# State-space weights made in the feed-forward block, untiled output products, and a weight block between all steps of the last attention

## The chip, the cores and the metric

The kernel runs on one core of one Trainium2 chip. The metric is device time in microseconds (us). The engines are PE (matrix products; PEld is its weight load), DVE (vector), ACT (scalar), POOL (GpSimd) and SP, which issues most transfers. SBUF is the memory beside the engines, PSUM the one that PE writes.

## The reference

The input is 512 tokens of 1024 features in float32. Two blocks follow each other, each of two layers. The first block (`block1`) mixes two attentions with gated projections. A layer of the second block is three residual steps: a gated feed-forward step of inner width 2816 (step 0), a token mixer (step 1), a second feed-forward step (step 2), each between RMS norms scaled by a vector made from `c`.

The mixer projects to `u` (512 wide), `q`, `k`, `v` (512 each), a forget logit and two gates. Its first branch is a state-space layer:

```python
lam_bar = jnp.exp(lam * dt)
b_bar = ((lam_bar - 1.0) / lam)[..., None] * b
bu = jnp.einsum('blgn,gpn->blgp', uf.astype(jnp.complex64), b_bar)
_, states = lax.associative_scan(combine, (a_all, bu), axis=1)
y = jnp.real(jnp.einsum('gnp,blgp->blgn', c, states)) + d_skip * uf
```

It has 32 groups of 16 channels with 64 complex states each. `gelu(y) @ glu_w` is split in a value and a gate. The second branch is a causal attention of 8 heads with a forget bias. Both branches are gated, added and projected.

## The kernel before

Every large product keeps float32 accuracy by three products of float32r parts: activations and weights are each split in a high part and a residual (`mm3`, lines 340 to 342; `tokens`, lines 417 to 419). A weight block of 128x1024 is loaded by SP (line 320), ACT makes its high part (line 323) and DVE its residual (line 324). Three buffers each hold raw, high and low parts; other tiles of up to 128x1024 share the buffers called `big`, 34 of them.

The program is written as Python generators that interleave work, and a planner orders each engine's instructions from that text and from estimated costs when the kernel is built. On the chip each engine follows its own list in that order.

A feed-forward step (`ffn`) runs over the 22 inner chunks of 128 in passes of 8, 7 and 7 (`SPLIT_K`). In a pass each chunk takes two weight blocks (`mblock`, 48 products of 512 columns) and an activation chain: tanh on ACT (line 1059), two DVE operations (1060, 1061), the high part on ACT (429), the residual on DVE or POOL (432). The pass ends with `tokens` for four groups of 128 tokens, whose results are added to `y` by DVE (1083). Between these, `pump` steps the job that makes the scaling vectors (line 1005, `modw` loads).

After pass 0 of step 0, `ssm_params` computes the small tables of the state-space layer. The mixer (`mixer`) projects `u` and `q`, then walks `fox_in` (forget logit, `k`, `v`) and `fox` (the attention). After every step of these, `side` advances three things: the state-space generator `ssm`, the 16 gate blocks in pairs, and, late, the 8 gated products (`gated`).

`ssm` treats the 512 tokens as 128 blocks of four (j = 0..3) and the channels in four quarters q. Per quarter it does this:

- DVE makes `bl`, the discretised input weights, in six operations (lines 1229 to 1234); PE turns them (line 1254) and ACT and DVE copy the result to `gt`.
- POOL makes `cl`, the output weights times powers of the transition (lines 1224, 1266, 1269), and `cs`, cosines and sines (1229 to 1234 with POOL as the engine).
- PE makes `kt`, the kernel within a block (1284, 1287), masked by DVE (1290).
- PE multiplies `u` by `gt` (1298); DVE and POOL rotate, DVE scans (1309, 1310), DVE and POOL rotate back to `hh`.
- PE makes the output in `yps`: four products with `kt` (1329) and 32 with 32 columns of `cl` each (1334). A tanh form of gelu follows (1338 to 1342), then the split in two parts (`gl`).

`halves_qk` (lines 561 to 573) splits a pair of heads for the scores (PE lines 579, 580) at the start of each pair.

## Time and profile before

| | |
|---|---|
| median of 3 runs | 3258.12 us (3255.19 to 3262.57) |
| profiled execution | 3255.03 us |
| its span, first to last instruction | 3253.0 us |
| mean granted clock of PE | 0.991 |

The span is what the rows are taken from; 2.0 us of the profiled execution lie around it. Busy time of an engine is not what limits the kernel by itself: it has to be read stage by stage, with what each engine waits for.

### The profile page before, as it was taken

The page shows a single profiled execution, that of the slowest core. Times are in us where ns is not written, and L with a number is a line of the kernel's source. Part 1 is how long each engine was busy: PE and PEld are TensorE (multiplying, and loading weights), DVE is VectorE, ACT ScalarE, POOL GpSimd, SP SyncE. Part 2 cuts the span into 40 slices and gives each one's busy share as a digit, 9 for nine tenths or more (in the row PEclk, how much of TensorE's full clock was granted, in tenths as well). Part 3 has the DMA queues.
Part 4 walks back from the last instruction along what each step waited for, and adds up shares of the span by engine and source line. Part 5 has one row for each costly group of instructions (what it writes and reads, how often), then busy time and mean ns, then how long its engine had stood idle before and what let it go on. Part 6 is the DMA issues. An engine that isn't in the chain of part 4 may idle for free. (4 is left out here: it accounts for less than half of the span.)

```text
span 3253.0 us, 41737 instructions
## 1 busy us (share of the span) xinstructions
PE 3159.7 (97%) x15958; PEld 2571.7 (79%) x15958; DVE 1961.7 (60%) x3525; ACT 1209.4 (37%) x2082; POOL 519.3 (16%) x578
## 2 busy tenths in 40 slices
PE   9999999999999999998999999999999989999999
PEld 8777888778788888876778888888888767788887
DVE  5897756887856848577565533634345776653334
ACT  4446423455333314433443222432234334442312
POOL 1200132000230101354001000100003451010000
PEclk9999999999999999999999999999999999999999
DMA  4243532233526537321233632332233211322323
GB/s 166 82 148 102 182 133 80 88 132 115 210 85 207 197 119 247 98 91 40 72 130 105 200 104 97 137 110 82 94 136 105 82 56 56 133 94 97 128 66 109
DMA packets 133464, 383.15 MB, mean 118 GB/s; under 512 B 15072, under 2 KB 21776, under 8 KB 133264
## 3 DMA queue, kind: packets, MB, share of 16 engines
q1 hardware_dynamic: 132208, 377.31, 34.2%
q0 software_dynamic: 1056, 3.17, 0.3%
q8 instruction: 126, 2.06, 0.3%
q14 instruction: 74, 0.61, 0.1%
HBM read 361.52 MB, written 18.90 MB: 117 GB/s over the span
## 5 line engine op out<-in xcount | busy, mean ns | idle before, releaser
L340 PE MATMUL acc<-big,wh 128*128 128x512 f32 (+1 forms) x2760 | 1074.4, 389 | 6.1 <-DVE tmp L725 2.9
L341 PE MATMUL acc<-big,wh 128*128 128x512 f32 (+1 forms) x2760 | 1068.9, 387 | 0.7 <-POOL big L517 0.7
L342 PE MATMUL acc<-big,wl 128*128 128x512 f32 (+1 forms) x2760 | 1066.1, 386 | 1.0 <-DVE wl L324 1.0
L324 DVE TENSOR_TENSOR wl<-raw,wh 128x1024 fp32r<-128x1024 f32 x396 | 500.7, 1267 | 527.9 <-ACT wh L323 511.9
L323 ACT CAST wh<-raw 128x1024 fp32r<-128x1024 f32 x396 | 414.1, 1046 | 978.6 <-issue 469.3
L340 PEld LDWEIGHTS acc<-big,wh 128*128 128x128 f32 x2760 | 521.2, 189 | 119.0 <-PE acc L342 5.3
L342 PEld LDWEIGHTS acc<-big,wl 128*128 128x128 f32 x2760 | 521.3, 189 | 109.0 <-DVE wl L324 1.4
L341 PEld LDWEIGHTS acc<-big,wh 128*128 128x128 f32 x2760 | 521.1, 189 | 103.6 <-POOL big L517 1.1
L1005 DVE SCALAR_TENSOR_TENSOR ms<-ms,big 128x512 f32<-128x512 f32 x288 | 199.6, 718 | 44.3 <-DMA ms<-in_modw_dram 43.7
L432 POOL TENSOR_TENSOR big<-tmp,big 128x512 fp32r<-128x512 f32 (+1 forms) x44 | 69.8, 1587 | 814.5 <-ACT big L429 814.5
L1061 DVE SCALAR_TENSOR_TENSOR tmp<-tmp,acc 128x512 f32<-128x512 f32 (+1 forms) x88 | 57.2, 650 | 149.9 <-PE acc L342 149.6
L429 ACT ACTIVATE big<-tmp 128x512 fp32r<-128x512 f32 (+1 forms) x148 | 88.1, 595 | 148.7 <-POOL tmp L881 56.3
L324 DVE TENSOR_TENSOR big<-raw,big 128x1024 fp32r<-128x1024 f32 x92 | 115.0, 1262 | 13.2 <-ACT big L323 12.5
L417 PE MATMUL acc<-big,big 128*128 128x512 f32 x288 | 113.1, 393 | 0.0
L419 PE MATMUL acc<-big,big 128*128 128x512 f32 x288 | 113.0, 392 | 0.0
L418 PE MATMUL acc<-big,big 128*128 128x512 f32 x288 | 112.9, 392 | 0.0
L605 ACT ACTIVATE big<-att,sm 128x512 f32<-128x512 f32 (+2 forms) x112 | 69.5, 624 | 116.6 <-DVE sm L603 116.4
L419 PE MATMUL att<-big,big 128*128 128x512 f32 x288 | 112.4, 390 | 0.0
L417 PE MATMUL att<-big,big 128*128 128x512 f32 x288 | 112.2, 390 | 0.0
L418 PE MATMUL att<-big,big 128*128 128x512 f32 x288 | 112.1, 389 | 0.0
L323 ACT CAST big<-raw 128x1024 fp32r<-128x1024 f32 x92 | 94.7, 1044 | 45.1 <-DMA raw<-in_w_dram 45.1
L482 ACT ACTIVATE hf<-big 128x512 f32<-128x512 f32 x80 | 50.3, 629 | 136.0 <-DVE big L1096 80.7
(395 smaller groups left out, 5102.4 us busy)
## 6 DMA issues: line engine op xcount, KB each, us to landing
raw<-in_w_dram SPq DMA_DIRECT2D x486, 512.0 KB, 3.3
ms<-in_modw_dram SPq DMA_DIRECT2D x288, 256.0 KB, 3.8
xb2l0s<-big SPq DMA_DIRECT2D x12, 512.0 KB, 2.7
big<-xb2l0s SPq DMA_DIRECT2D x12, 512.0 KB, 7.0
xb1l<-big SPq DMA_DIRECT2D x8, 512.0 KB, 2.6
big<-xb1l SPq DMA_DIRECT2D x8, 512.0 KB, 6.3
xb2l1s<-big SPq DMA_DIRECT2D x8, 512.0 KB, 2.6
big<-xb2l1s SPq DMA_DIRECT2D x8, 512.0 KB, 7.0
```

Source lines behind the costliest of these rows:

```text
L323: nc.scalar.copy(hi[:, :n], raw[:, :n])
L324: nc.vector.tensor_tensor(lo[:, :n], raw[:, :n], hi[:, :n].bitcast(F32), op=ALU.subtract)
L340: nc.tensor.matmul(ps, lhsT=hi, rhs=a, start=first, stop=False)
L341: nc.tensor.matmul(ps, lhsT=hi, rhs=b, start=False, stop=False)
L342: nc.tensor.matmul(ps, lhsT=lo, rhs=a, start=False, stop=last)
L417: nc.tensor.matmul(ps[m], lhsT=a, rhs=hi, start=c == o[0], stop=False)
L418: nc.tensor.matmul(ps[m], lhsT=a, rhs=lo, start=False, stop=False)
L419: nc.tensor.matmul(ps[m], lhsT=b, rhs=hi, start=False, stop=c == o[-1])
L429: nc.scalar.activation(hi, src, AF.Copy, scale=scale)
L432: eng.tensor_tensor(lo, src, hi.bitcast(F32), op=ALU.subtract)
L605: nc.scalar.activation(ps[j], s_ps[j], AF.Exp, bias=ng[:, j:j + 1], scale=scale, accum_out=rs[:, j:j + 1])
L1005: nc.vector.scalar_tensor_tensor(w, in0=w, scalar=0.5, in1=self.sc[m], op0=ALU.mult, op1=ALU.mult, accum_out=sums[:, n, m:m + 1])
```

## The change

1. `ssm_prep` makes the state-space weights inside feed-forward step 0 of the same layer. All three complex products (`bl`, `cl`, `cs`) are now on DVE. The finished tiles go to DRAM (`ssd`) by transfers that POOL issues, 11 per quarter. The generator has 40 steps: in pass 0 and pass 3 one step follows each chunk, in passes 1 and 2 two, and two follow each token group.
2. Step 0 runs in passes of 5, 5, 5 and 7; `pump` there does half as many job steps after a chunk.
3. The kernel within a block is stored as a 128x128 triangle of 32x32 blocks per group of 32 channels, so that the output needs 12 products of 128x128 per quarter. The gelu's result goes to DRAM and back (`yd`), five transfers from POOL, to return to the order of the tokens.
4. `ssm` in the mixer loads five tiles per quarter by SP and keeps only the work that needs `u`.
5. `fox` yields after each pair of score blocks, 24 times in all, and `fill` puts one gate block or gated product after each; `fox_in` is followed only by `ssm` steps. `halves_qk` for the next pair is called earlier.
6. `big` has 37 buffers; the memory for them comes from the scratch of POOL's transfers, set to 2048.

```diff
-SPLIT_K = (8, 7, 7)
+SPLIT_K = ((5, 5, 5, 7), (8, 7, 7))
-MIX = (1, 3, 1, 16)
-BUFS = dict(raw=3, wh=3, wl=3, big=34, tmp=5, hf=3, ms=5, s16=8, pw=1, pr=1, acc=3, att=2, aux=2, yps=1, mod=2, sums=1)
+BUFS = dict(raw=3, wh=3, wl=3, big=37, tmp=5, hf=3, ms=5, s16=8, pw=1, pr=1, acc=3, att=2, aux=2, yps=1, mod=2, sums=1)
...
-    c[:, C_BLK:C_BLK + 128] = (q // 32 == k // 32).astype(f)
+    c[:, C_BLK:C_BLK + 128] = (q % 32 == k).astype(f)
...
-        for p, n in enumerate(SPLIT_K):
+        prep = self.ssm_prep(l) if i == 0 else iter(())
+        for p, n in enumerate(SPLIT_K[i // 2]):
...
-                self.pump(2)
+                for _ in range(1 if p % 3 == 0 else 2):
+                    next(prep, None)
+                self.pump(1 if i == 0 else 2)
...
-            if p < len(SPLIT_K) - 1:
+            if p < len(SPLIT_K[i // 2]) - 1:
...
                     self.pump()
+                    for _ in range(2):
+                        next(prep, None)
...
-                if i == 0:
-                    self.ssm_p = self.ssm_params(l)
+        for _ in prep:
+            pass
...
+        P.update(rho=r[:, 3], tc=tc_, ts=ts_, l=(lr, li), f=(fr, fi))
+
+    def ssm_prep(self, l):
...
+        P = {}
+        for _ in self.ssm_params(l, P):
+            yield 1
...
+        s4 = [128, 4, 8, 16]
+        self.ssd[l] = ssd = self.dr.tile([4, 4, 128, 1024], F32, name=f"ssd{l}")
+        t = self.big()
+
+        def cplx(o, a, b, c, d, view, sign):
+
+            plus = (ALU.subtract, ALU.add)[::sign]
+            for k, x, y in ((0, c, d), (1, d, c)):
+                v.tensor_tensor(view(o[:, k]), a, x, op=ALU.mult)
+                v.tensor_tensor(view(t[:, k]), b, y, op=ALU.mult)
+                v.tensor_tensor(o[:, k], o[:, k], t[:, k], op=plus[k])
+                yield 1
+
+        def store(i, o, eng=g):
+            eng.dma_start(ssd[q, i], o.rearrange("p a b -> p (a b)"))
 
         for q in range(4):
             pq = slice(q * 4, q * 4 + 4)
             bk = self.big()
-            bc, kt = v3(bk[:, 0]), v3(bk[:, 1])
+            bc = bk[:, 0].rearrange("p (a b) -> p a b", a=4)
+            kt = bk[:, 1, 0:128].rearrange("p (a b) -> p a b", a=4)
             nc.sync.dma_start(bk[:, 0], self.io["ssmbc"][l, q])
...
+            for _ in cplx(bl, b0, b1, f0, f1, lambda x: x.rearrange("p (a b c) -> p a b c", a=4, b=4), 1):
+                yield 1
...
+            nc.scalar.mul(bc[:, 3], bc[:, 3], -1.0)
+            cl = self.big()
...
+            for _ in cplx(cl, l0, l1, c0, c1, lambda x: x.rearrange("p (a b c) -> p a b c", a=4, b=4), -1):
+                yield 1
+            store(1, cl)
+            yield 1
...
-            nc.scalar.mul(bc[:, 3], bc[:, 3], -1.0)
-            cl = self.big()
-            t = self.big()
...
-            mul(v4(t[:, 0]), cv[1], lv[1])
...
+            store(0, gt)
+            yield 1
             cs = self.big()
...
-            cplx(g, cs, *ta, *tb, lambda t: t.rearrange("p (a b c) -> p a b c", a=4, b=8))
...
+            it = cplx(cs, *ta, *tb, lambda x: x.rearrange("p (a b c) -> p a b c", a=4, b=8), 1)
+            yield next(it)
...
+            ps = self.t("aux", [128, 512])
+            for i in range(4):
+                s = slice(i * 32, i * 32 + 32)
+                for c in range(2):
+                    w = bb[:, c * 128 + i * 32:c * 128 + i * 32 + 32]
+                    nc.tensor.matmul(ps[s, 0:32], lhsT=w, rhs=bc[:, 2 + c, s], start=c == 0, stop=c == 1)
+                for c in range(2):
+                    w = bb[:, c * 128 + i * 32:c * 128 + i * 32 + 32]
+                    nc.tensor.matmul(ps[s, 32:128], lhsT=w, rhs=cl[:, c, i * 128:i * 128 + 96],
+                                     start=c == 0, stop=c == 1)
+            nc.scalar.copy(bk[:, 1, 0:128], ps[:, 0:128])
+            yield next(it)
+            store(2, cs)
+            v.scalar_tensor_tensor(kt[:, 0], in0=self.cst[:, C_BLK:C_BLK + 32],
+                                   scalar=self.par[l][:, P_SD + q:P_SD + q + 1],
+                                   in1=kt[:, 0], op0=ALU.mult, op1=ALU.add)
+            rho = ru[:, 0].rearrange("p (a b) -> p a b", a=4)
             nc.scalar.copy(rho, P["rho"][:, pq].unsqueeze(2).to_broadcast([128, 4, 128]))
             g.memset(rho[:, :, 0:1], 0.0)
-            nc.sync.dma_start(ru[:, 1], ud[q])
+            tri = ssd[q, 3, :, 0:512].rearrange("p (i x) -> p i x", i=4)
+            for j in range(4):
+                js = slice(j * 32, j * 32 + 32)
+                g.dma_start(tri[js, :, j * 32:].rearrange("e i x -> i e x"), bk[:, 1, 0:128 - j * 32])
+                if j:
+                    g.dma_start(tri[js, :, 0:j * 32],
+                                self.cst[js, C_BLK + 32:C_BLK + 32 + j * 32].unsqueeze(1).to_broadcast([32, 4, j * 32]))
+            g.dma_start(ssd[q, 3, :, 512:1024], ru[:, 0])
             yield 1
-            ps = self.t("aux", [128, 512])
-            for c in range(2):
-                nc.tensor.matmul(ps[:, 0:128], lhsT=bb[:, c * 128:(c + 1) * 128], rhs=bc[:, 2 + c],
-                                 start=c == 0, stop=c == 1)
-            for c in range(2):
-                nc.tensor.matmul(ps[:, 128:512], lhsT=bb[:, c * 128:(c + 1) * 128], rhs=cl[:, c, 0:384],
-                                 start=c == 0, stop=c == 1)
...
-            v.tensor_tensor(kt, v3(ps), blk, op=ALU.mult)
...
+    def ssm(self, l, ud, out):
...
+        def load(q):
+
+            ts = [self.big() for _ in range(4)]
+            for i, t in enumerate(ts):
+                nc.sync.dma_start(t.rearrange("p a b -> p (a b)"), self.ssd[l][q, i])
+            uu = self.big()
+            nc.sync.dma_start(uu[:, 1], ud[q])
+            return *ts, uu
+
+        for q in range(4):
+            gt, cl, cs, kr, uu = load(q)
+            ct, st = cs[:, 0], cs[:, 1]
+            yield 1
...
             yield 1
+            yield 1
-            uq = u[q // 2][:, q % 2]
-            for a in range(4):
-                n = (4 - a) * 128
-                nc.tensor.matmul(y_ps[:, a * 128:], lhsT=kt[:, a], rhs=uq[:, :n], start=a == 0, stop=False)
-            for j in range(4):
-                o = y_ps[:, j * 128:(j + 1) * 128]
+            for i in range(4):
+                s = slice(i * 128, (i + 1) * 128)
+                nc.tensor.matmul(y_ps[:, s], lhsT=kr[:, 0, s], rhs=uu[:, 1, s], start=True, stop=False)
                 for c in range(2):
-                    for i in range(4):
-                        nc.tensor.matmul(o[i * 32:(i + 1) * 32], lhsT=cl[:, c, j * 128 + i * 32:j * 128 + i * 32 + 32],
-                                         rhs=hh[:, c, i * 128:(i + 1) * 128], start=False, stop=j == 3 and c == 1)
+                    nc.tensor.matmul(y_ps[:, s], lhsT=cl[:, c, s], rhs=hh[:, c, s], start=False, stop=c == 1)
...
-            out.append(self.split(q2.rearrange("p (j k) -> p k j", j=4), scale=0.5, view="p (k j) -> p k j"))
+
+            g.dma_start(yd[q], q2)
+            d = yd[q].rearrange("(j e) (i k) -> j e i k", j=4, i=4)
+            for i in range(4):
+                g.dma_start(uu[i * 32:(i + 1) * 32, 0].rearrange("e (j k) -> e j k", j=4),
+                            d[:, :, i].rearrange("j e k -> e j k"))
+            yield 1
+            out.append(self.split(uu[:, 0].rearrange("p (j k) -> p k j", j=4), scale=0.5, view="p (k j) -> p k j"))
             yield 1
...
+        def fill():
+
+
+            for j in range(8):
+                t = self.big()
+                tg.append(t)
+                for k in range(2):
+                    ps = self.mblock(self.wk("gate"), h)
+                    nc.scalar.activation(t[:, k], ps, AF.Tanh, scale=0.5)
+                    yield 1
+            for _ in S_:
+                pass
...
-        def side(i):
-
-            while side.s * MIX[0] < i + 1 and next(S_, None):
-                side.s += 1
-            while len(tg) < 8 and len(tg) * MIX[1] < i + 1:
-                tg.append(self.g_pair(h))
-            while len(gl) == 4 and side.g < len(tg) and side.g * MIX[2] < i + 1 - MIX[3] and next(G_, None):
-                side.g += 1
...
+        S_ = self.ssm(l, ud, gl)
+        F_ = fill()
         next(S_)
-        n = 0
-        for it in (self.fox_in(l, h, st), self.fox(st, yb)):
-            for _ in it:
-                side(n)
-                n += 1
-        for _ in S_:
-            pass
-        for _ in G_:
+        for n, _ in enumerate(self.fox_in(l, h, st)):
+            for _ in range(1 + n % 2):
+                next(S_, None)
+        for n, _ in enumerate(self.fox(st, yb)):
+            next(F_, None)
+            next(S_, None)
+        for _ in F_:
             pass
...
+        ahead = self.halves_qk(qf[0][:, 0], kf[0][:, 0])
         for hp in range(4):
-            qk = self.halves_qk(qf[hp // 2][:, hp % 2], kf[hp // 2][:, hp % 2])
+            qk = ahead
...
-                    if q == 2:
-                        yield 1
+                    if q and e and hp < 3:
+                        n = hp + 1
+                        ahead = self.halves_qk(qf[n // 2][:, n % 2], kf[n // 2][:, n % 2])
+                    yield 1
...
-    nc = bacc.Bacc("TRN2", target_bir_lowering=False, num_devices=1)
+    nc = bacc.Bacc("TRN2", target_bir_lowering=False, num_devices=1, dynamic_dma_scratch_size=2048)
```

## Rows read from the trace of the kernel before

**Rows 1.** The page, its first part: busy time, share of the span, instructions.

```profile
PE 3159.7 (97%) x15958; PEld 2571.7 (79%) x15958; DVE 1961.7 (60%) x3525; ACT 1209.4 (37%) x2082; POOL 519.3 (16%) x578
```

**Rows 2.** Windows by stage: feed-forward 0, mixer, of each layer; columns in the prediction.

```profile
922.80:1300.60 377.80, 374.70 (x1763) 311.24 (x1763) 244.01 (x581) 121.03 (x176) 44.27 (x64) 0.99 0.52 178
1300.60:1713.50 412.90, 389.42 (x2204) 311.57 (x2203) 275.73 (x385) 170.57 (x311) 119.11 (x109) 0.98 0.25 85
...
2086.20:2458.50 372.30, 371.55 (x1763) 308.56 (x1762) 164.00 (x318) 119.09 (x174) 33.91 (x47) 1.00 0.32 106
2458.50:2875.30 416.80, 391.92 (x2204) 311.69 (x2203) 275.51 (x381) 170.35 (x311) 118.45 (x109) 0.98 0.25 84
```

**Rows 3.** Waits of PE in the mixer of layer 0: total us, times, longest.

```profile
PE aux L1254 <- DVE big L1231: 5.7, 2, 3.4
PE att L580 <- DVE big L573: 3.9, 1, 3.9
PE aux L1254 <- DVE big L1234: 3.5, 2, 2.4
...
PE att L579 <- DVE big L570: 1.9, 1, 1.9
PE aux L1254 <- ACT big L928: 1.6, 1, 1.6
```

**Rows 4.** The same view, mixer of layer 1.

```profile
PE aux L1254 <- DVE big L1231: 6.6, 2, 3.5
PE aux L1254 <- DVE big L1234: 5.2, 3, 3.1
...
PE att L580 <- DVE big L573: 2.5, 1, 2.5
...
PE aux L1254 <- ACT big L928: 1.9, 1, 1.9
```

**Rows 5.** Windows of 10 us, the nine at a lower clock: first and last.

```profile
1400.00:1410.00 10.00, 6.97 (x26) 5.11 (x24) 10.00 (x7) 1.05 (x1) 10.00 (x7) 0.83 0.18 61
...
2690.00:2700.00 10.00, 8.73 (x40) 6.41 (x41) 9.58 (x17) 1.86 (x6) 3.08 (x3) 0.83 0.16 52
```

**Rows 6.** Timeline of PE, layer 0: start us, duration us, instruction.

```profile
1360.96 2.05 PE L1298 MATMUL att<-big,big 128*128 128x128 f32 x16
...
1363.08 0.39 PE L341 MATMUL acc<-big,wh 128*128 128x512 f32 x1
1363.31 0.39 PE L342 MATMUL acc<-big,wl 128*128 128x512 f32 x1
```

**Rows 7.** Timeline of PE, one quarter's output products, layer 1.

```profile
2545.31 2.32 PE L1329 MATMUL yps<-big,big 128*128 128x512 f32 x8
2548.21 0.43 PE L1334 MATMUL yps<-big,big 128*32 128x128 f32 x8 [0.57 <-DVE big L1322]
2548.80 1.74 PE L1334 MATMUL yps<-big,big 128*32 128x128 f32 x56 [0.17 <-DVE big L1323]
```

**Rows 8.** Lines 1231 and 1234, whole run: duration ns min/median/max, first, last.

```profile
L1231 DVE TENSOR_TENSOR big<-big,big x8: 1480/1562/1747, 1347.7 to 2666.3; 128x512 f32<-128x512 f32 x8
...
L1234 DVE TENSOR_TENSOR big<-big,big x8: 676/1538/1770, 1352.9 to 2672.4; 128x512 f32<-128x512 f32 x8
```

**Rows 9.** Groups by line, DVE, feed-forward 0 of layer 0.

```profile
L1005 DVE SCALAR_TENSOR_TENSOR ms<-ms,big 128x512 f32<-128x512 f32 x108 | 77.6, 749 | 27.5 <-DMA ms<-in_modw_dram 27.3
L324 DVE TENSOR_TENSOR wl<-raw,wh 128x1024 fp32r<-128x1024 f32 x50 | 62.0, 1242 | 43.9 <-ACT wh L323 43.4
...
L1060 DVE SCALAR_TENSOR_TENSOR tmp<-tmp,acc 128x512 f32<-128x512 f32 (+1 forms) x22 | 14.2, 644 | 4.9 <-ACT tmp L1059 4.9
```

**Rows 10.** Line 1029, a transfer issued from POOL.

```profile
L1029 POOL DMA_DIRECT2D gates<-tmp x6: 587/600/747, 1065.8 to 3013.5; - x6
...
DMA to landing us min/median/max: 1.6/1.7/1.8
```

More of the change, by code (lines that the diff above doesn't have):

```diff
@@ L1208, in ssm_params @@
             v.tensor_tensor(fi[:, :, j], d1, d2, op=ALU.add)
-        return dict(rho=r[:, 3], tc=tc_, ts=ts_, l=(lr, li), f=(fr, fi))
-    def ssm(self, l, P, u, ud, out):
+        P.update(rho=r[:, 3], tc=tc_, ts=ts_, l=(lr, li), f=(fr, fi))
+    def ssm_prep(self, l):
         nc = self.nc
         v, g = nc.vector, nc.gpsimd
+        P = {}
+        for _ in self.ssm_params(l, P):
+            yield 1
         d4 = [128, 4, 4, 32]
-        def v4(t):
-            return t.rearrange("p (a b c) -> p a b c", a=4, b=4)
-        def v3(t):
-            return t.rearrange("p (a b) -> p a b", a=4)
-        def mul(o, a, b):
-            g.tensor_tensor(o, a, b, op=ALU.mult)
-        def cplx(e, o, a, b, c, d, view):
-            t = self.big()
-            e.tensor_tensor(view(o[:, 0]), a, c, op=ALU.mult)
-            e.tensor_tensor(view(t[:, 0]), b, d, op=ALU.mult)
-            e.tensor_tensor(o[:, 0], o[:, 0], t[:, 0], op=ALU.subtract)
-            e.tensor_tensor(view(o[:, 1]), a, d, op=ALU.mult)
-            e.tensor_tensor(view(t[:, 1]), b, c, op=ALU.mult)
-            e.tensor_tensor(o[:, 1], o[:, 1], t[:, 1], op=ALU.add)
+        s4 = [128, 4, 8, 16]
[10 more added lines that the diff above has]
+            eng.dma_start(ssd[q, i], o.rearrange("p a b -> p (a b)"))
         for q in range(4):
@@ L1275, in ssm @@
-            ct, st = cs[:, 0], cs[:, 1]
-            ru = self.big()
-            rho = v3(ru[:, 0])
+            store(0, gt)
+            yield 1
+            cs = self.big()
+            ta = [x[:, pq, 16:24].unsqueeze(3).to_broadcast(s4) for x in (P["tc"], P["ts"])]
+            tb = [x[:, pq, 0:16].unsqueeze(2).to_broadcast(s4) for x in (P["tc"], P["ts"])]
+            it = cplx(cs, *ta, *tb, lambda x: x.rearrange("p (a b c) -> p a b c", a=4, b=8), 1)
+            yield next(it)
+            ps = self.t("aux", [128, 512])
@@ new lines, in ssm_prep, with v3, mul @@
+            g.dma_start(ssd[q, 3, :, 512:1024], ru[:, 0])
+            yield 1
+    def ssm(self, l, ud, out):
+        nc = self.nc
+        v, g = nc.vector, nc.gpsimd
+        yd = self.dr.tile([4, 128, 512], F32, name=f"yd{l}")
+        def v3(t):
+            return t.rearrange("p (a b) -> p a b", a=4)
+        def mul(o, a, b):
+            g.tensor_tensor(o, a, b, op=ALU.mult)
+        def load(q):
[9 more added lines that the diff above has]
+            yield 1
@@ L1347, in mixer @@
         nc, par = self.nc, self.par[l]
-        P = self.ssm_p
         h = self.acts(h)
@@ L1371, in mixer @@
         gl, yb, tg = [], [], []
-        def gated():
+        def fill():
[5 more added lines that the diff above has]
+                    nc.scalar.activation(t[:, k], ps, AF.Tanh, scale=0.5)
+                    yield 1
+            for _ in S_:
+                pass
             for j in range(8):
@@ L1383, in gated @@
                 yield 1
-        def side(i):
-            while side.s * MIX[0] < i + 1 and next(S_, None):
-                side.s += 1
-            while len(tg) < 8 and len(tg) * MIX[1] < i + 1:
-                tg.append(self.g_pair(h))
-            while len(gl) == 4 and side.g < len(tg) and side.g * MIX[2] < i + 1 - MIX[3] and next(G_, None):
-                side.g += 1
-        side.s = side.g = 0
-        S_ = self.ssm(l, P, u, ud, gl)
-        G_ = gated()
-        next(S_)
-        n = 0
-        for it in (self.fox_in(l, h, st), self.fox(st, yb)):
-            for _ in it:
-                side(n)
-                n += 1
-        for _ in S_:
-            pass
-        for _ in G_:
+        S_ = self.ssm(l, ud, gl)
+        F_ = fill()
+        next(S_)
+        for n, _ in enumerate(self.fox_in(l, h, st)):
[5 more added lines that the diff above has]
+        for _ in F_:
             pass
@@ L1419, in mixer @@
         return self.stage(f"b2l{l}s1", self.rows("mo", 8), mg, lambda t, ps: self.add(t, ps, gate), nxt)
-    def g_pair(self, h):
-        t = self.big()
-        for k in range(2):
-            ps = self.mblock(self.wk("gate"), h)
-            self.nc.scalar.activation(t[:, k], ps, AF.Tanh, scale=0.5)
-        return t
     def fox_in(self, l, h, st):
@@ L1516, in run @@
         self.mod = [None] * DEPTH
+        self.ssd = [None] * DEPTH
         self.gates = [self.dr.tile([3, D], F32, name=f"gates{l}") for l in range(DEPTH)]
```

34 lines of the change are left out of this document (12 added, 22 removed).

## The prediction, written before the changed kernel was run

> **What bounds the kernel now.** The first part of the page comes first: PE is busy for 97% of the span, DVE for 60%, POOL for 16% [rows 1]. So time comes off only where PE has less to do, or where it stands still or runs slowly. The second view is the table of windows, cut where the last output product of each stage ends. Its columns are the stretch, its length, busy time of PE, PEld, DVE, ACT and POOL, the granted clock, DMA share and GB/s [rows 2]. The two feed-forward steps that the change touches hold 374.7 us of PE in 377.8 and 371.6 in 372.3: dense. The two mixers hold 389.4 in 412.9 and 391.9 in 416.8: PE stands still for 23.5 and 24.9 us there. The third view says for what. In layer 0 the transposes of `bl` (line 1254) wait 5.7 + 3.5 + 1.6 = 10.8 us [rows 3], in layer 1 6.6 + 5.2 + 1.9 = 13.7 [rows 4], mostly for DVE's complex products. The first scores of a head pair (579, 580) wait 3.9 + 1.9 and 2.5 + 1.9, together 10.2 us, for residuals that DVE makes late behind the same products [rows 3, 4] (the row of line 570 reads the same in both mixers and stands once).
>
> The fourth view is the mixers in windows of 10 us. Nine of them show a granted clock below 0.9; in the two that stand here it is 0.83, and in both DVE is busy for 9.5 us or more [rows 5]. Each follows one of the waits above: five a wait of line 1254, four a wait of a head pair. 0.83 is the mean of full speed and of half, 1.2 GHz, in part of the window: it takes 1.7 us of work from it. That makes 8.5 us behind the transposes and 6.8 behind the head pairs.
>
> **The change, part by part.** *Weights out of the mixer.* The transposes' 24.5 us of waiting have no place left in the mixer, and with them go the 8.5 us at low clock: 33.0. The transposes themselves, 32 a layer, and the products for the kernel within a block only change place; the latter go from 8 records a quarter to 32 shorter ones, and I count them as equal. *Head pairs.* DVE's list in the mixer loses a quarter's six products four times (and two masking operations), and the next pair is split earlier. All of it gone would be 10.2 + 6.8 = 17.0 us; none gone is the other end. The first pair still stands at the entry to `fox` with nothing put before it, so I take half, 8.5.
>
> *Output products.* One quarter costs 2.32 + 0.43 + 1.74 = 4.49 us of PE [rows 7]. The 12 new products have the form of line 1298, whose 16 records took 2.05 us, 0.128 us each [rows 6]; the four products of line 1329 leave eight records, two each, so 12 leave 24 and take 3.07. The gain is 1.42 us a quarter, 11.4 over eight. If they ran as slowly as those of line 1329 (0.29 a record, with up to 512 columns [rows 7]) they would cost 6.96 and lose 19.8 over eight: that is the other end, far, since line 1298 has the very shape.
>
> *The same work in feed-forward 0.* Each quarter brings DVE 18 operations of 128x512. The nearest rows are the same operations on DVE before: lines 1231 and 1234 have medians of 1.56 and 1.54 us, and a fastest of 0.68 [rows 8]. The medians were taken while POOL made `cl` and `cs` from SBUF beside them, in the stretches where both engines are full (10.0 us of 10 in the first of [rows 5]); POOL is busy for 44 of 378 us in feed-forward 0 [rows 2]. So 72 operations a layer cost between 49 us at 0.68 and 112 at 1.56, and I take a value near the lower end, 60. Layer 0 carries DVE 244.0 us there [rows 2]. The halved pump takes away 19 x 2 job steps and the extra pass gives 4 x 2 back: 30 steps of 0.75 us, 22 [rows 9]. They move to step 2, which has DVE free. The extra pass adds eight additions to `y`, 5 us at the 0.64 of line 1060 [rows 9]. This gives 244 + 60 - 22 + 5 = 287 of 378 us (at most 339), and 164 + 65 = 229 of 372 in layer 1: the weight residuals and PE cover it. If that cover failed, each wait would be PE time.
>
> The Trainium skill, page SBUF — State Buffer, section Who interferes with whom, says that a DVE instruction with two SBUF inputs and a GpSimd instruction that reads SBUF exclude each other, and the later one waits. By it the 72 operations cost 49 us where POOL is idle, and the median of [rows 8] where it is not; the trace agrees, 0.68 against 1.56. The sum below would be the same at 49 us as at 60.
>
> *Pass ends.* The fifth chunk's parts are needed (4 x 3 + 2 x 3) products of 0.23 us [rows 6] after the token groups begin, 4.1 us; in a pass of seven it is 30 products, 6.9. Its chain has three DVE operations of about 0.64 [rows 9], and a preparation operation ahead of any of them adds 0.68 to 1.56. I take 1.3 us for each of three such pass ends in two layers, 8 us, with 0 and 28 (a step of three slow operations, 4.7 us, each time) as its ends.
>
> *Queues.* POOL issues 44 transfers a layer in feed-forward 0 and 20 in the mixer. At 0.60 us each [rows 10] that is 26 and 12 us; each waits for the tile that it stores, and behind it on POOL stand the residuals of every second chunk, due only at the pass end. In the mixer the trip of `yd` adds five issues and two landings of 1.7 us [rows 10], some 6.4 us a quarter, to a chain that nobody waits for until the gated products. SP gets 20 loads a layer, issued a step ahead; weights behind them have three raw buffers in hand. For new waits of these kinds in the mixers I take 5 us, between 0 and 20.
>
> The sum against the profiled execution: -33.0 - 8.5 - 11.4 + 8 + 5 = -39.9, so 3255.0 becomes 3215. The median of the runs shown lies 3.1 us above that execution, so I forecast 3218.
>
> **The rivals.** *The waits travel with the work.* PE's list is fixed when the kernel is built, and the transposes now stand among the dense products of feed-forward 0. If the plan sets them as early as it did in the mixer, PE waits there as it did here. Then the 33.0 us stay, and the sum is -7: 3251. For it speaks that all 24.5 us were a plan that was too early for DVE; against it that DVE has idle time there and POOL stays out of its way.
>
> *DVE binds in feed-forward 0: slower.* A pass of five holds 5 x 48 + 120 products, 360 x 0.23 = 83 us of PE. In pass 1 of layer 0 DVE has 15 residuals of 1.24 [rows 9], 18.6; 13 us of chains and additions; 18 job steps of 0.75, 13.5; and 18 of the 40 preparation steps, 36 operations. At 0.68 these are 24 us, 70 in all, and nothing binds. At 1.56 they are 56, and 101 in all: PE lacks 18 us in that pass. Layer 1, without the job, lacks 5 (88); pass 2, with 12 steps left, just nothing (82). Every late residual can put PE at half clock as in [rows 5]; half of the 30 in these two passes at 1.7 us each are 25. The sum is -40 + 18 + 5 + 25 = +8: 3266. It decides from a mean operation of (83 - 45) / 36 = 1.06 us on; from about 1.5 us the whole gain is eaten.
>
> *The output's trip comes late.* The first gated product needs all four quarters. It stands 16 gate blocks after `fox` begins, 6 blocks of 24 products, 33 us, after the last step of `ssm`. If the four chains run 33 us later than written, PE stands still for up to 20 us a mixer, and the sum is about zero: 3258. The Trainium skill, the same page, section A bandwidth-pool intuition that's wrong, gives 620 ns for a transfer issued by GpSimd alone and 3100 ns beside a DVE copy; by it the five issues of a quarter would take 15.5 us instead of the 3 of [rows 10], an estimate that makes this rival likelier; the one row here shows 0.75 at most.
>
> **How the numbers follow.** Forecast 0.64, waits travel 0.15, DVE binds 0.13, the trip late 0.08. The forecast's own range is 3198 to 3240: all waits of the head pairs gone and no new ones (-61), or none gone and 16 us more of new ones. The range for 8 in 10 adds the first and third rival at its upper side and all terms at their best, 3192 to 3257, and leaves out the case where DVE binds. A measurement of this kernel tells about 0.2%, 6.5 us, from no change. Faster: 0.64 and two thirds of the travelling waits, 0.74. The same: the rest of these and most of the late trips, 0.12. Slower: DVE binding and the worst late trips, 0.14.
>
> **What would show it.** The windows of the mixers should fall to about 390 us each with a clock of 0.99 or 1.00 and no line of transposes among PE's waits; those of feed-forward 0 should stay within 384 and 377. DVE's preparation operations should last 0.7 to 0.9 us. A quarter's output products should take about 3 us. It would be wrong if transposes or weight residuals head PE's waits in feed-forward 0, if DVE's operations there last over 1.1 us, or if the gated products wait for `gl`.

## The result, and the profile after

The changed kernel takes 3276.51 us (median of 5 runs, 3276.24 to 3287.03), the kernel before beside it 3258.12. The ratio is 1.0062, 95% interval 1.0052 to 1.0073: slower by 0.6%, where 3218 and faster were forecast. The profiled execution has a span of 3275.9 us. Its windows by stage, columns as in [rows 2]:

```profile
923.90:1328.80 404.90, 388.29 (x1923) 319.89 (x1923) 268.02 (x602) 126.08 (x195) 64.02 (x94) 0.98 0.49 166
1328.80:1733.70 404.90, 372.91 (x1947) 306.50 (x1946) 228.37 (x345) 162.88 (x295) 56.62 (x77) 0.96 0.32 110
2106.40:2493.00 386.60, 381.94 (x1924) 315.04 (x1923) 217.57 (x407) 126.07 (x194) 59.05 (x82) 1.00 0.37 126
2493.00:2898.20 405.20, 371.95 (x1947) 305.97 (x1946) 228.46 (x345) 163.06 (x295) 56.69 (x77) 0.96 0.32 110
```

Against [rows 2] feed-forward 0 grew by 27.1 and 14.3 us and the mixers fell by 8.0 and 11.6. The mixers are the surprise. PE's work there did shrink (389.4 and 391.9 busy before, 372.9 and 372.0 now, although more of it ran slowly: the granted clock is 0.96 where it was 0.98). But PE now stands still for 32.0 and 33.2 us of a mixer, where it stood 23.5 and 24.9. Its waits in the mixer of layer 0 (total us, times, longest; layer 1 reads the same within 1 us):

```profile
PE yps L1379 <- DVE big L1369: 7.5, 2, 4.9
PE att L578 <- ACT big L604: 6.3, 2, 3.2
PE att L1345 <- DMA big<-ud: 5.9, 1, 5.9
PE att L579 <- DVE big L572: 3.2, 1, 3.2
PE att L578 <- DVE big L569: 2.6, 1, 2.6
```

The transposes of `bl` (line 1254 in [rows 3]) are gone from this list, as forecast. In their place stand the output products (1379), which wait for `hh`; the third quarter's first products (1345), which wait for its loads; and at the entry to `fox` the first scores (578, 579), for the split halves and then for the exponentials (604). The timeline of PE shows these last in one stretch of 21 us (start us, duration us, instruction, the wait before it in brackets):

```profile
1476.34 3.44 PE L1345 MATMUL att<-big,big 128*128 128x128 f32 x16 [5.87 <-DMA big<-ud]
1482.60 0.66 PE L578 MATMUL att<-big,big 128*128 128x128 f32 x2 [2.60 <-DVE big L569]
1486.50 0.45 PE L579 MATMUL att<-big,big 128*128 128x128 f32 x1 [3.24 <-DVE big L572]
...
1491.09 0.69 PE L578 MATMUL att<-big,big 128*128 128x384 f32 x1 [3.08 <-ACT big L604]
```

No product of a weight block stands among them: the stretch between two waits holds a few short scores. The 16 products of line 1345 take 3.44 us after their wait, where the same 16 took 2.05 in [rows 6]. The windows of 10 us over that place show why:

```profile
1468.80:1478.80 10.00, 4.13 (x19) 3.50 (x18) 2.51 (x3) 4.45 (x7) 0.00 (x0) 0.68 0.82 322
1478.80:1488.80 10.00, 3.38 (x17) 2.76 (x15) 9.77 (x10) 0.00 (x0) 5.88 (x4) 0.67 0.00 0
1488.80:1498.80 10.00, 7.71 (x37) 6.89 (x38) 6.89 (x17) 4.44 (x12) 0.40 (x2) 0.62 0.01 2
```

PE is busy for 4.1, 3.4 and 7.7 us of 10, and the granted clock is 0.62 to 0.68: most of the stretch runs at 1.2 of 2.4 GHz. Before, a wait cost one window of 0.83 [rows 5]. Here windows of 1 us show the clock back at 1.00 only from 1479.8 to 1481.8 us, after the first of the four waits, and then at 0.50 from 1482.8 to 1495.8. A low clock costs nothing while PE stands still, so its price is read from busy time: with the old layout (`m_mixold`, below) about as many records keep PE busy for 367.9 and 368.2 us where they take 372.9 and 372.0 here, some 5 and 4 us a mixer. The larger part of what is lost is standing still.

The wait for `ud` is a matter of SP's queue, shown by its timeline: the weight loads ahead of the quarter's loads held SP until 1467.5 us, and `ud`, issued last, landed as PE's wait ended, at 1476.3.

```profile
1454.81 12.59 SPq L319 DMA_DIRECT2D raw<-in_w_dram  x3
1467.49 1.83 SPq L1331 DMA_DIRECT2D big<-ssd  x4
1469.38 0.44 SPq L1333 DMA_DIRECT2D big<-ud  x1
```

In feed-forward 0 PE has new work, the transposes and the products for the kernel within a block. Their groups, layer 0 (busy, mean ns of one | idle before them):

```profile
L1273 PE MATMUL aux<-cst,big 128*128 128x128 f32 x32 | 4.3, 274 | 2.7 <-DVE big L1237 2.7
...
L1294 PE MATMUL aux<-big,big 128*32 128x96 f32 x64 | 3.8, 247 | 0.0
L1291 PE MATMUL aux<-big,big 128*32 128x32 f32 x64 | 3.1, 201 | 4.8 <-DVE big L1277 4.8
```

That is 11.2 us of products (11.0 in layer 1), and 7.5 us of waits for them in layer 0. They are not all: PE stands still there for 16.6 us, where it stood 3.1 before, and the second place among its waits is taken by weight residuals (total us, times, longest):

```profile
PE acc L341 <- DVE wl L323: 3.9, 2, 2.9
```

DVE's preparation operations themselves are fast (min/median/max ns, the third of each product):

```profile
L1237 DVE TENSOR_TENSOR big<-big,big x48: 679/684/1784, 1022.9 to 2348.6; 128x512 f32<-128x512 f32 x48
```

The median is 684 ns, the low end of the range taken from [rows 8]. But in the second pass of layer 0 DVE is busy for 86.4 us of 98.4 (the first window; the second is the same pass in layer 1):

```profile
1014.90:1113.30 98.40, 89.98 (x443) 71.92 (x442) 86.41 (x190) 28.59 (x43) 19.56 (x35) 0.98 0.59 198
```

```profile
2192.70:2283.50 90.80, 88.68 (x444) 70.84 (x443) 59.53 (x82) 26.82 (x39) 19.57 (x33) 1.00 0.46 156
```

### The profile page after: what moved, and what is told of

Its sections match the earlier page's. It is cut to its first block, busy times and chain, and to the rows that moved or that the text cites. A ratio compares the mean times of both kernels' runs of the same rounds, so it can differ in the third digit from the quotient of the medians.

```text
span 3275.9 us, 41755 instructions
## 1 busy us (share of the span) xinstructions
PE 3147.8 (96%) x15766; PEld 2576.7 (79%) x15766; DVE 1967.5 (60%) x3631; ACT 1207.7 (37%) x2090; POOL 454.7 (14%) x608
## 5 line engine op out<-in xcount | busy, mean ns | idle before, releaser
L323 DVE TENSOR_TENSOR big<-raw,big 128x1024 fp32r<-128x1024 f32 x86 | 108.2, 1271 | 14.1 <-ACT big L322 14.0
L416 PE MATMUL acc<-big,big 128*128 128x512 f32 x264 | 105.5, 399 | 4.8 <-ACT big L322 4.8
L417 PE MATMUL acc<-big,big 128*128 128x512 f32 x264 | 104.3, 395 | 0.5 <-DVE big L323 0.5
L416 PE MATMUL att<-big,big 128*128 128x512 f32 x264 | 104.5, 396 | 0.0
L418 PE MATMUL acc<-big,big 128*128 128x512 f32 x264 | 104.1, 394 | 0.0
L418 PE MATMUL att<-big,big 128*128 128x512 f32 x264 | 103.6, 392 | 0.0
L417 PE MATMUL att<-big,big 128*128 128x512 f32 x264 | 103.5, 392 | 0.0
L601 DVE TENSOR_REDUCE sm<-att 128x1 f32<-128x512 f32 (+3 forms) x150 | 87.7, 595 | 25.4 <-PE att L1533 23.2
```

Of the source, the lines that this page charges most:

```text
L323: nc.vector.tensor_tensor(lo[:, :n], raw[:, :n], hi[:, :n].bitcast(F32), op=ALU.subtract)
L416: nc.tensor.matmul(ps[m], lhsT=a, rhs=hi, start=c == o[0], stop=False)
L417: nc.tensor.matmul(ps[m], lhsT=a, rhs=lo, start=False, stop=False)
L418: nc.tensor.matmul(ps[m], lhsT=b, rhs=hi, start=False, stop=c == o[-1])
L601: nc.vector.tensor_reduce(m[:, j:j + 1], s_ps[j], axis=AX.X, op=ALU.max)
```

## The experiments

Two questions: why the mixers did not fall to their work, and what layer 0's feed-forward pays over the 11.2 us. For the first, **theory A**: the last attention's new layout takes the gate blocks out of `fox_in` (before, a pair at every third step from the first on), and runs the state-space steps there at 1.5 a step, so PE meets chains that are not ready with nothing to do meanwhile. Its rival, **theory B**: the trips through DRAM are late wherever the blocks stand. Each kernel was timed in three rounds beside the kernel before; ratios are to it, with 95% intervals.

**`m_mixold`: the changed kernel, attention laid out as before.** `fill` is replaced by `gated`, `side` and `g_pair` of the kernel before, `fox` by its old form.

```diff
+MIX = (1, 3, 1, 16)
...
-        for n, _ in enumerate(self.fox_in(l, h, st)):
-            for _ in range(1 + n % 2):
-                next(S_, None)
-        for n, _ in enumerate(self.fox(st, yb)):
-            next(F_, None)
-            next(S_, None)
...
+        for it in (self.fox_in(l, h, st), self.fox(st, yb)):
+            for _ in it:
+                side(n)
+                n += 1
...
```

> The changed kernel with the last attention laid out as before: gate pairs every third step from the first on, one state-space step per step, steps of `fox` only after its second score group, each head pair split at its own start. Theory A (lost cover: the gate blocks that stood between the steps of `fox_in` now all stand in `fox`, and the state-space steps run 1.5 per step, so PE meets chains that are not ready and falls to half clock): mixers fall from 405 to 385-392 us each and the clock there from 0.96 to 0.98 or more, time 3236-3250. Theory B (the waits come from the trips through DRAM, which are late wherever the blocks stand): mixers stay at 400-410, time 3268-3280. Feed-forward 0 stays at 405 and 386 by both.

Measured: 3240.63 us, ratio 0.9943 (0.9926 to 0.9959). The windows of its two mixers:

```profile
1331.70:1714.80 383.10, 367.86 (x1947) 300.97 (x1946) 228.40 (x345) 162.74 (x296) 55.86 (x77) 0.99 0.34 116
2474.60:2859.50 384.90, 368.20 (x1948) 301.47 (x1947) 229.55 (x345) 162.65 (x295) 56.44 (x77) 0.99 0.34 115
```

They are 21.8 and 20.3 us shorter than with the new layout, idle for 15.2 and 16.7 us in place of 32.0 and 33.2, at 0.99 of the clock. The trips through DRAM are all still there, so theory B falls. Putting the old layout back turns the change from 0.6% slower to 0.6% faster.

**`b_fill`: the kernel before with only the new layout** (with one state-space step per step, since its quarter has other steps).

```diff
...
-        for it in (self.fox_in(l, h, st), self.fox(st, yb)):
-            for _ in it:
-                side(n)
-                n += 1
...
+        for n, _ in enumerate(self.fox_in(l, h, st)):
+            next(S_, None)
+        for n, _ in enumerate(self.fox(st, yb)):
+            next(F_, None)
+            next(S_, None)
...
```

> The kernel before with only the last attention's layout of the changed kernel: gate and gated blocks only between the 24 steps of `fox`, next head pair split ahead, one state-space step per step as before. Theory A: the mixers get longer by 5 to 15 us each, time 3268-3290, with waits in `fox_in` and at the entry to `fox`. Theory B: the early split takes the head pairs' waits away and nothing else changes: 5 to 8 us less in each mixer, time 3242-3250.

Measured: 3285.52 us, ratio 1.0078 (1.0063 to 1.0093), mixers of 427.8 and 431.2 us: 14.9 and 14.4 longer than [rows 2]. Its first waits in layer 0:

```profile
PE yps L1334 <- DVE big L1322: 9.7, 2, 5.2
PE aux L1254 <- DVE big L1231: 8.2, 3, 4.1
PE aux L1254 <- DVE big L1234: 6.9, 3, 3.1
```

The same chains as in [rows 3], each later for PE: the wait for `hh` (line 1322), 1.2 us in layer 0 before and 0.57 in layer 1 [rows 7], is now up to 5.2 and 5.9. The layout costs by itself, without any of the rest.

**`m_pace`: the changed kernel, one state-space step per step of `fox_in`.**

```diff
-            for _ in range(1 + n % 2):
-                next(S_, None)
+            next(S_, None)
```

> The changed kernel with one state-space step per step of `fox_in` in place of 1.5. If the pace is what makes the chain of a quarter late (theory A, its part 1), the waits of the output products for line 1369 (7.5 us a mixer) and of the third quarter's products for `ud` (5.9 and 6.7) go, with 5 to 10 us of low clock: mixers 385-395, time 3245-3258. If the bare entry to `fox` is what matters (part 2), only the first goes: mixers 396-400, time 3258-3268. By theory B nothing goes: 3270-3280.

Measured: 3251.66 us, ratio 0.9976 (0.9966 to 0.9986); mixers 393.1 and 390.0 us. The wait for `ud` is gone and one of the two for line 1369; the other stays at 4.9 us, with one of 4.6 at the entry to `fox`, and 8.3 us of waits for the probabilities are new. The pace, in the stretch without blocks, is the larger part of the loss in the mixers: 27.0 of 42.1 us (810.1 in the changed kernel, 783.1 here, 768.0 in `m_mixold`). The next run takes up the other 15.1.

**`m_spread`: blocks at all steps, some of them in `fox_in`.**

```diff
         for n, _ in enumerate(self.fox_in(l, h, st)):
-            for _ in range(1 + n % 2):
-                next(S_, None)
+            next(S_, None)
+            if n % 2 or n == 8:
+                next(F_)
         for n, _ in enumerate(self.fox(st, yb)):
-            next(F_, None)
+            if n > 13 or n % 3 != 1:
+                next(F_, None)
             next(S_, None)
```

> The changed kernel with all its parts, blocks between all steps of `fox` too, but five of the 24 gate and gated blocks moved forward into `fox_in` (one at every second step and one ahead of `fox`), five steps of `fox` left without one, and one state-space step per step. Theory A (bare `fox_in`): the waits for line 1369, for `ud`, and at the entry to `fox` go, mixers 382-388 as with the old layout, time 3236-3246. Rival (blocks between all steps of `fox` and the early split are themselves harmful): mixers 392-400, time 3250-3268.

Measured: 3241.33 us, ratio 0.9945 (0.9930 to 0.9959); mixers 387.2 and 386.4, together 9.5 us less than `m_pace` and 5.6 more than `m_mixold`. The mixers of `b_split` (below) differ by more than that from [rows 2] with no edit in them, so no harm shows from the 24 steps of `fox` or from the early split; what costs is the pace and a `fox_in` that has no block left. No run keeps the pace of 1.5 with blocks in `fox_in`, so the pace alone is not priced there. Nor do the new parts gain over the old layout: PE's waits for the exponentials stay, 7.6 us in layer 0 here against 5.8 in `m_mixold`.

**`f_pump`: the modulation job out of the middle passes of feed-forward 0.**

```diff
-                self.pump(1 if i == 0 else 2)
+                self.pump(2 if i or p % 3 == 0 else 0)
...
-                    self.pump()
+                    self.pump(1 if i or p == 0 else 0)
```

> The changed kernel with the modulation job taken out of the two middle passes of feed-forward 0 (where the preparation runs two steps per chunk) and at its old pace in the first and last. If DVE's list with the job is what makes PE wait in layer 0 (15.9 us over what the moved products cost, against 3.0 in layer 1 that has no job), feed-forward 0 of layer 0 falls from 405 to 390-395 and the time to 3262-3268. If not, it stays within 3 us of 405: 3273-3280. The mixers and layer 1 do not change.

Measured: 3279.01 us, ratio 1.0059 (1.0044 to 1.0074); layer 0's feed-forward 0 at 405.5 us. The theory's forecast missed, but the test is weak: 13 job operations still ran in the second pass, DVE was busy for 79.9 of its 97.4 us, and PE's first wait for the preparation there, 2.9 us, stayed. The waits of line 1291 fell from 4.8 to 1.0 us, and those for high parts of weights grew from 2.1 to 4.4.

**`b_split`: the kernel before with the extra pass alone.**

```diff
-SPLIT_K = (8, 7, 7)
+SPLIT_K = ((5, 5, 5, 7), (8, 7, 7))
```

> The kernel before with feed-forward 0 in passes of 5, 5, 5 and 7 chunks and nothing else changed: the price of the extra pass. By the prediction's term 8 us for both layers, between 0 and 28: feed-forward 0 at 378 to 392 and 372 to 386, time 3258-3286, likeliest 3266. If the price of a pass end shows only with the preparation beside it, feed-forward 0 stays within 2 us of before and the time within 0.2%.

Measured: 3266.71 us, ratio 1.0021 (1.0011 to 1.0030). Its feed-forward 0:

```profile
922.80:1305.40 382.60, 376.17 (x1763) 309.23 (x1763) 246.92 (x591) 120.15 (x176) 39.11 (x63) 1.00 0.52 176
2096.80:2469.50 372.70, 372.23 (x1763) 308.58 (x1762) 169.95 (x327) 118.83 (x174) 31.90 (x46) 1.00 0.31 106
```

4.8 and 0.4 us over [rows 2], together 5.2, and 6.4 by the medians (3266.71 against 3260.32): near the 8 us that the prediction took for the pass ends, and inside its ends. How far one trace can be trusted shows in the same execution: its mixers, where DVE, ACT and POOL run the same instructions in the same order as before, take 418.7 and 420.8 us, 5.8 and 4.0 over [rows 2].

The four runs that follow, and `x_ahead`, have the old layout of `m_mixold`, whose feed-forward 0 takes 405.2 and 386.3 us. Five kernels with the same code there gave 404.9 to 410.5 in layer 0, so a few us decide nothing.

**`x_act`: the copy of `bb` on ACT later.** Theory C: ACT stands at that copy for DVE, and weight splits queue behind it.

```diff
             nc.sync.dma_start(bk[:, 0], self.io["ssmbc"][l, q])
+            nc.scalar.mul(bc[:, 3], bc[:, 3], -1.0)
...
-            nc.scalar.copy(bb.rearrange("p (c a b) -> p c a b", c=2, a=4),
-                           bl.rearrange("p c (a j b) -> p c a j b", a=4, j=4)[:, :, :, 3])
-            nc.scalar.mul(bc[:, 3], bc[:, 3], -1.0)
...
             store(1, cl)
             yield 1
+            nc.scalar.copy(bb.rearrange("p (c a b) -> p c a b", c=2, a=4),
+                           bl.rearrange("p c (a j b) -> p c a j b", a=4, j=4)[:, :, :, 3])
```

> The run with the last attention's old layout, plus: in the preparation the sign of `bc` is turned as soon as it lands, and the copy of `bb` on ACT stands after the products of `cl` instead of before. Theory C (ACT stands at the copy of `bb` for DVE's product, 31.0 us over seven times in the changed kernel, and the weight splits queued behind it come late for PE): feed-forward 0 of layer 0 falls from 405 by 5 to 12 us and that of layer 1 by 0 to 3, time 3226-3236. Rival (the wait is DVE's own list, with the job and the residuals, and ACT only shows it): no change, 3238-3243.

Measured: 3243.4 us, ratio 0.9947 (0.9932 to 0.9962); 408.5 us in layer 0. Inconclusive: ACT still stood at the copy for 29.3 us (31.0 in the changed kernel), so the wait was not taken away and theory C was not tried.

**`x_split`: passes of 8, 7 and 7.** Theory D: short passes with the preparation beside them make weights and residuals late.

```diff
-SPLIT_K = ((5, 5, 5, 7), (8, 7, 7))
+SPLIT_K = ((8, 7, 7), (8, 7, 7))
...
-                for _ in range(1 if p % 3 == 0 else 2):
+                for _ in range(2):
                     next(prep, None)
```

> The run with the last attention's old layout, with passes of 8, 7 and 7 in feed-forward 0 in place of 5, 5, 5 and 7 and two preparation steps after every chunk. If the extra pass costs what the prediction took for it, it falls by 4 us a layer: 3230-3236. If short passes are what makes weights and residuals late in layer 0 (theory D), that feed-forward falls from 405 to 390-395: 3222-3230. If the denser preparation hurts more than the pass helps: 3241-3255.

Measured: 3227.25 us, ratio 0.9902 (0.9886 to 0.9919): 1.0% faster than the kernel before. Its four stages:

```profile
923.20:1314.60 391.40, 383.96 (x1923) 315.92 (x1923) 265.70 (x594) 127.53 (x196) 66.54 (x95) 1.00 0.51 171
1314.60:1699.30 384.70, 370.96 (x1947) 303.73 (x1946) 228.61 (x345) 162.68 (x295) 55.88 (x77) 0.98 0.34 115
2072.00:2459.70 387.70, 383.21 (x1924) 316.47 (x1923) 213.79 (x398) 127.03 (x194) 56.91 (x83) 1.00 0.37 126
2459.70:2845.00 385.30, 368.25 (x1947) 301.18 (x1946) 229.44 (x345) 162.78 (x295) 56.45 (x77) 0.99 0.33 115
```

Feed-forward 0 of layer 0 falls by 13.8 us, of which the extra pass alone explains 4.8 (`b_split`). The rest comes from the passes and the preparation steps together: this run changes both, since the steps now stand two after every chunk. Layer 1 does not fall (387.7).

**`f_even`: the preparation thinner in the middle passes**, 5, 5, 5 and 7 kept.

```diff
-                for _ in range(1 if p % 3 == 0 else 2):
-                    next(prep, None)
+                next(prep, None)
```

> The run with the last attention's old layout, with one preparation step after every chunk of feed-forward 0 in place of two in the middle passes (two after each token group as before), so that the preparation reaches into the last pass. If its density in the second pass (DVE busy for 86 of 98 us there) is what costs layer 0 its 11 us beyond moved products and extra pass, that feed-forward falls from 405 to 394-400 and the time to 3228-3236. If the extra pass with any preparation beside it costs them, 403-407 and 3238-3243.

Measured: 3230.7 us, ratio 0.9909 (0.9890 to 0.9927); feed-forward 0 at 398.3 and 384.9 us. The density of the steps is part of it: layer 0 is 6.9 us below `m_mixold`, and below all five kernels above.

**`f_nope`: without the preparation's work on PE.** The transposes and the kernel's products are left out; their results are replaced by copies of `bl` and `cl`.

```diff
-                ps = self.t("aux", [128, 512])
-                for i in range(4):
-                    s = slice(i * 128, (i + 1) * 128)
-                    nc.tensor.transpose(ps[:, s], bl[:, c, s], self.ident)
+                ps = bl[:, c]
...
-            nc.scalar.copy(bk[:, 1, 0:128], ps[:, 0:128])
+            nc.scalar.copy(bk[:, 1, 0:128], cl[:, 0, 0:128])
```

> The run with the last attention's old layout, with the preparation's work on TensorE left out: `gt` is copied from `bl` without the transposes and the kernel within a block from `cl` without its products, so the outputs are not those of the reference. By the busy times of those lines in the changed kernel (4.3 + 3.8 + 3.1 us and 4.1 + 3.8 + 3.1) each feed-forward 0 falls by 11 us, to 394 and 375, and the time to 3218. If PE's waits for this work are what costs layer 0 the rest, it falls by 18 to 24 there, to 382-387, and the time to 3206-3212.

Measured: 3210.1 us, ratio 0.9852 (0.9837 to 0.9866):

```profile
925.60:1312.40 386.80, 378.08 (x1764) 311.69 (x1763) 266.10 (x602) 126.25 (x195) 67.74 (x94) 0.99 0.52 173
2072.50:2446.30 373.80, 372.58 (x1764) 308.59 (x1763) 216.98 (x407) 126.46 (x194) 60.25 (x82) 1.00 0.39 130
```

18.4 and 12.5 us less than `m_mixold`: in layer 1 the products themselves, 11.0, and little more; in layer 0 7.2 us more than its 11.2. That is the second of the two outcomes expected: with the products go PE's waits for them. All of DVE's preparation is still there, so by these traces DVE's work, with the rest of the preparation, costs PE some 4.2 us in layer 0 (386.8 against the 382.6 of `b_split`) and 1.1 in layer 1.

**`x_ahead`: the early split in the old layout, gated products one step later.**

```diff
-MIX = (1, 3, 1, 16)
+MIX = (1, 3, 1, 17)
...
+        ahead = self.halves_qk(qf[0][:, 0], kf[0][:, 0])
         for hp in range(4):
-            qk = self.halves_qk(qf[hp // 2][:, hp % 2], kf[hp // 2][:, hp % 2])
+            qk = ahead
...
+                    if q and e and hp < 3:
+                        n = hp + 1
+                        ahead = self.halves_qk(qf[n // 2][:, n % 2], kf[n // 2][:, n % 2])
```

> The run with the last attention's old layout, plus the early split of the next head pair, and the gated products one step later (17 in place of 16). The waits for lines 570 and 573 (2.9 us a mixer) and the one wait of 4.1 and 3.5 us of the gated products for the last quarter's residual go, with up to 2 us of low clock each: mixers 376-381 in place of 383 and 385, time 3226-3236. If the waits only move on to the exponentials of the softmax (5.8 and 7.4 us): 3237-3243.

Measured: 3241.72 us, ratio 0.9941 (0.9926 to 0.9956); mixers 387.1 and 385.9. The waits named went (0.7 us is left of the gated products'), and those for the exponentials grew from 5.8 to 12.2 us in layer 0 and from 7.4 to 12.3 in layer 1: PE's waiting is only handed on.

**`x_entry`: the best of all parts** (`m_spread`, passes of 8, 7 and 7, and the first pair split earlier).

```diff
+        st["qk"] = self.halves_qk(st["q"][0][:, 0], st["k"][0][:, 0])
         for j in range(4):
             self.to_tokens(self.mblock(self.wk("v"), h), st["v"], j)
...
-        ahead = self.halves_qk(qf[0][:, 0], kf[0][:, 0])
+        ahead = st["qk"]
```

> The same layout as in the run above, plus passes of 8, 7 and 7 in feed-forward 0, and the first head pair split between the keys and the values instead of at the start of `fox`. If the three effects add: mixers 376-384, feed-forward 0 at 391 and 388, time 3212-3228. If the waits of the softmax's exponentials stay whatever stands around them: mixers 384-388, time 3226-3234.

Measured: 3225.67 us, ratio 0.9898 (0.9882 to 0.9915); mixers 385.8 and 386.2. Not to be told from `x_split`; both beat the kernel before by 1.0% and the changed one by about 1.5%.

## Why the prediction was wrong, step by step

**The step that failed** is the term for new waits in the mixers, "I take 5 us, between 0 and 20". It looked for them in the queues, and the new layout of the attention had no term of its own: neither that the gate blocks leave `fox_in` nor that the state-space steps there run at 1.5 a step was costed; the early split was the only part of it that was. Measured, the layout costs 42.1 us in the two mixers of the changed kernel (810.1 us against the 768.0 of `m_mixold`), waits and low clock together: 27.0 go with the pace (`m_pace`), 9.5 with the missing blocks (`m_spread`), and the other 5.6 are no more than executions differ by. In the kernel before, at its own pace, the layout costs 29.3 (`b_fill`). The 42.1 are more than the whole gain forecast. The chains of [rows 3] waited little because blocks stood around them: in `b_fill` the same chains without these blocks wait longer. Only one of the new waits is a queue's, that for `ud` (5.9 and 6.7 us), and there the quarter's loads stood behind weights, where the prediction looked for weights behind the quarter's loads.

The four stages came out 61.7 us above the sum (+21.8 by [rows 2] against -39.9). Of these 42.1 are the layout. Feed-forward 0 holds 11.2: it grew by 41.4, of which 22.2 are the moved products (the mixers, by the count of equal, lost as much) and 8 the pass ends of the sum. The other 8.4 lie in the mixers and stay with the old layout.

**The transposes' waits, 33.0 us.** Right in the mixers: no wait of the transposes of `bl` is left there (those of `v`, line 922, wait for 3.3 us in layer 0). The rival of the travelling waits came in part: 7.5 us of waits for the moved work in layer 0 of feed-forward 0 and 1.0 in layer 1. By the prediction's own sign, transposes or weight residuals at the head of PE's waits there, it was wrong in layer 0: the first three places are 4.8 us for the new products, 3.9 for weight residuals and 2.7 for the transposes.

**Moved products, counted as equal.** Their groups keep PE busy for 11.2 and 11.0 us in feed-forward 0 (14.3 and 14.4 in the mixers before), so the forecast that these stages "stay within 384 and 377" contradicted the prediction's own count of equal: by it they should have read some 11 us more, and the mixers as much less. With the old layout the mixers do fall below 390, to 383 and 385.

**Head pairs, 8.5 us.** Not gained: PE waits for 5.8 us in layer 0 and 6.0 in layer 1, all of it for the first pair, together 11.8 against the 10.2 before. The term lay at its other end, and the waits for exponentials would have taken the gain (`x_ahead`).

**Output products, 11.4 us.** Right, a little better: in the trace of the changed kernel two records of line 1377 and four of 1379 follow each other at 0.67 us, four times a quarter, 2.7 us in place of the 3.07 forecast and the 4.49 of [rows 7].

```profile
1414.53 0.39 PE L1377 MATMUL yps<-big,big 128*128 128x128 f32 x2
1414.76 0.61 PE L1379 MATMUL yps<-big,big 128*128 128x128 f32 x4
1415.20 0.39 PE L1377 MATMUL yps<-big,big 128*128 128x128 f32 x2
```

**Pass ends, 8 us.** About right where they stand alone (5.2 us by the windows of `b_split`). In layer 0 with the preparation beside them, passes and steps together cost 13.8 (`x_split`). The step behind it, DVE's load of the second pass, was taken as 70 us at 0.68 an operation; it was 86.4 with operations of that very duration. Into it fell 50 operations of complex products where 36 were reckoned, and 53 small ones of `ssm_params`, which had been left out. So by the number of operations, not by their duration, DVE's list passed the 83 us of PE that the rival set against it; but with a list of 79.9 us (`f_pump`) the pass was hardly shorter, 97.4 us, so this load is not shown to be what makes it long. Part of the loss is the density of the steps (`f_even`), and 7.2 us of it go with the preparation's products on PE (`f_nope`). Which wait starts it stays open, since `x_act` did not remove the one suspected, and neither did `f_pump`.

**DVE binds.** Its condition, 1.06 us for a mean operation, was not met: 0.68. The Trainium skill, page SBUF — State Buffer, section Who interferes with whom, says that a DVE instruction with two SBUF inputs contends with a GpSimd instruction that reads SBUF. The trace agrees: the median is 684 ns with POOL mostly idle, and the slowest of the 48 operations, 1784 ns, stood beside a residual on POOL.

```profile
1046.58 2.08 POOL L431 TENSOR_TENSOR big<-tmp,big 128x512 fp32r<-128x512 f32 x1 [4.47 <-ACT big L428]
...
1047.42 1.78 DVE L1237 TENSOR_TENSOR big<-big,big 128x512 f32<-128x512 f32 x1
```

**The trip late.** No product waited for `gl` in the changed kernel; in `m_mixold` one did, for 4.1 and 3.5 us. The Trainium skill, the same page, section A bandwidth-pool intuition that's wrong, gives about 3100 ns for a transfer that GpSimd issues beside a DVE copy. No run here shows it: the eight stores of `yd` took 599 to 664 ns, but none of them stood beside a DVE copy (four beside no DVE operation, two beside a weight residual, two beside the scalings of line 1540).

Taken together, feed-forward 0 and the mixers of `x_split` are 30.7 us shorter than [rows 2] (1549.1 against 1579.8). The forecast for these parts, without pass ends, would have been 47.9: the parts gave about two thirds of it, and one rearrangement that the forecast did not price, with one extra pass in a full stretch, cost more than they gave.

## What to carry to other kernels

When a change moves the filler, not only the work, list for each stretch what stands between a chain's start and its first reader before and after, and price the stretch that loses its blocks and any chain that is stepped faster there. Change the layout last: here the same change without it was 0.6% faster, and with the old passes as well 1.0%. A part that costs little alone (the extra pass, 4.8 us) has to be priced again beside the work that is put into the same stretch.

## What was not expected of the hardware

A row of short waits costs more than its sum. In the changed kernel's layer 0 four waits of 2.6 to 5.9 us, 14.8 us in all, stand within 21 us. The granted clock was 0.62 to 0.68 over the three windows of 10 us around them; from the second wait on it stayed at 0.50 for 13 us, with waits of 2.6, 3.2 and 3.1 us there and short scores between them. About half of the low clock fell on time in which PE stood still, so by windows of 1 us it cost some 5 us of work on top of the 14.8; a single wait of [rows 5] cost 1.7. While PE stood among dense products (feed-forward 0 of layer 1, waits of at most 1.4 us) the clock stayed at 1.00.
